# One more pair of chunks as seven block products, tables made once, and a longer split lead in a two-layer decoder kernel

## The chip, the cores and the metric

The kernel runs on one core of a Trainium2 chip. A core has a matrix engine (TensorE, PE in the profile), a vector engine (VectorE, DVE), a scalar engine (ScalarE, ACT), a general engine (GpSimd, POOL) and a queue for transfers (SyncE, SP). Each engine works through its own instructions in order and waits on semaphores for the others. The metric is the time of one execution in microseconds; the kernel before has a median of 1203.88 us over 3 runs (1203.52 to 1204.22).

## The reference

The program is a decoder trunk of two layers over 256 tokens of width 1024. Each layer adds four sub-layers to the residual h, each behind an RMS norm with its own gain:

```python
for l in range(DEPTH):
    h = h + 0.5 * swiglu(rms_norm(h, ffn1_norm[l]), ffn1_w_gate[l], ffn1_w_up[l], ffn1_w_down[l])
    h = h + hybrid_mixer(rms_norm(h, mix_norm[l]), ...)        # state-space groups beside attention
    h = h + memory_cross_attention(rms_norm(h, xattn_norm[l]), rms_norm(mem, mem_norm[l]), ...)
    h = h + 0.5 * swiglu(rms_norm(h, ffn2_norm[l]), ffn2_w_gate[l], ffn2_w_up[l], ffn2_w_down[l])
return rms_norm(h, final_norm)

def swiglu(x, w_gate, w_up, w_down):
    return (jax.nn.silu(x @ w_gate) * (x @ w_up)) @ w_down
```

The feed-forward width is 2816. The state-space part of the mixer has 32 groups of 64 complex states; from its parameters (decay, angle, step size, input and output matrices B and C) the kernel makes tables that depend on no token, and then uses them on all tokens.

## The kernel before, in words

**Precision.** Every large product is made of three: both operands are split into a high part (rounded for the fast matrix format) and a low part (the rest), and high x high, high x low and low x high are summed. So each weight has to be split on the chip. `split_unit` (line 582) makes the high part on ScalarE (`whi`) and the low part on VectorE (`wlo`), in halves of 512 columns, and multiplies by the norm's gain on the way where the plan says so. `split_whole` (line 525) does 1024 columns at once and no gain.

**The stream of weights.** `stream_plan` (line 104) lists every weight unit (128 x 1024) in the order of use. A unit is 12 matmuls of 512 columns: two halves, two blocks of 128 tokens, three products each. SyncE loads units into 4 raw buffers; the split parts have 5 buffers (`N_W`, line 34).

**The planner.** Python code writes all engines' instructions in one order, helped by a small model of time (`Clock`, line 171). TensorE's stream is the main line; everything else (evacuations, transposes, tables, the mixer's chains) is a generator that is resumed when the model's time has come. `feed` (line 503) issues splits ahead of the main line, until a unit is due more than `LEAD` = 4.0 of the model's microseconds later (line 37), or no split buffer is free. One unit is 2.56 of them (`STEP`, line 38, is a half). A generator that yields nothing comes back `MARGIN` = 0.2 after its last operation was to end (line 39).

**Feed-forward stages.** The width is cut into 11 chunks of 256; each has 4 gate/up units and 2 down units. `ffn` (line 857) takes one chunk after the other: the projection into PSUM (`mm`), then silu (`sg`) and the gated product (`g`), four transposes per chunk, a split into `gT`, and the down product into `acc`. `ffn_second` (line 948) is used for the second stage of each layer. There two pairs of chunks (2 and 3, 7 and 8) are made as seven products of blocks instead of eight: a pair is a 2 x 2 block product (token halves and halves of the inner width by two chunks), and with sums and differences of blocks (of the activations in `combos`, line 917, of the weights in `add_block`, line 543, of the products in `pair_step`, line 1010) seven products are enough. One block product is 2 units of 6 matmuls. The order of chunk units (P), block products (S) and down units (D) is written out by hand in `SECOND` (line 51). Since blocks of weights are added before they are split, the norm's gain cannot be in the weights there: `prep` (line 775), which finishes the residual and makes the next stage's input, multiplies it into the activations (`split_gain`, line 470).

**The mixer** (line 1329) projects with 16 w_in units and 12 wkv units; beside that stream run the state's chain (`ssm_states`, line 1373, with two scans and several rotations on VectorE, then `ssm_out`, line 1444, ending in `yT`) and the attention. The chain's result is needed by the units of w_glu.

**The tables** (`ssm_tables`, line 1145) are made once a layer as one generator. It has a small part, some 80 operations on 128 x 16 (exponentials by polynomial, angles, powers, `pw`, `fz`), and a big part: the rotations `rot` and decay `dt`, B scaled (`bbar`), V and its transposes `VT`, the output tables W, and the direct term `ks`, which is copied into `dt` by eight transfers on POOL's queue. For layer 1 it is spawned at 22.0 of the model's time (`START`, line 46), for layer 2 at 12.0 after that layer begins, that is inside its first feed-forward stage. `ssm_states` waits for the whole of it. Scratch tiles of 1024 words come from one pool of 12 (`s4t`, line 396), large table tiles from four named ones, which the pairs' weight blocks X and Y and the combined activations use too.

Of the kernel before, what the change touches and what calls it, by code (L numbers as in the profile page):

```python
# [36 lines left out]
LEAD = 4.0  # L37
STEP = 1.28
# [7 lines left out]
START = (22.0, 34.0)  # L46
# [8 lines left out]
)  # L55
# [13 lines left out]
def second_items():  # L69

    seen = {}
    for item in SECOND.split():
        k = seen[item] = seen.get(item, -1) + 1
        yield item[0], int(item[1:]), k
# [29 lines left out]
def stream_plan():  # L104

    plan = []
    for l in range(L):
# [10 lines left out]
        def second(nm):  # L118
            for kind, j, k in second_items():
                if kind == "P":  # L120
                    plan.append((nm + "_gu", l, 4 * j + k, "A", None, 4 if j == 0 else 1))
                elif kind == "D":
                    plan.append((nm + "_dn", l, 2 * j + k, "B", None, 1))
                else:
                    _, loads, operand, add = PAIR[k]
                    for u in range(2):
                        n = [4 * (j + a) + 2 * b + u for _, a, b in loads]
                        plan.append((nm + "_gu", l, n, "S", ((l, j), u, [x[0] for x in loads], operand, add), 1))
# [7 lines left out]
        ffn("ffn1")  # L136
# [20 lines left out]
    return plan, need  # L157


class Task:  # L160


    def __init__(self, gen, now):
        self.gen, self.t, self.done, self.waiters = gen, now, False, []
        self.pe = -1.0


class Clock:
# [73 lines left out]

    def engine(self, e, cost):
        t = self.cur
        start = max(self.busy[e], t.t + 0.13)
        self.busy[e] = start + cost
        t.t = start + cost
# [113 lines left out]
class Trunk:  # L361
    def __init__(self, ctx, tc, io):
# [21 lines left out]
        self.plan, self.need = stream_plan()  # L384
# [118 lines left out]
    def feed(self, least=-1):  # L503
# [353 lines left out]
    def ffn(self, nm, preps, tail):  # L857
# [4 lines left out]
        def evac(j):  # L862
            def f(t, ps):
# [17 lines left out]
                for f in range(2):  # L881
                    o = f * 256 + t * 128
                    self.p.transpose(p[:, o:o + 128], g[:, f * 128:f * 128 + 128], self.ident)
# [64 lines left out]
    def ffn_second(self, nm, preps, tail):  # L948
# [133 lines left out]
        for kind, j, k in second_items():  # L1082
# [19 lines left out]
            elif kind == "S":  # L1102
                pair_step(j, k)
            else:
# [13 lines left out]
    def exp_acc(self, out, x, n):  # L1118
# [5 lines left out]
        yield  # L1124
        v.tensor_scalar(k, k, -MAGIC, None, op0=ALU.add)
        v.scalar_tensor_tensor(r, k, -0.693359375, r, op0=ALU.mult, op1=ALU.add)
        yield
        v.scalar_tensor_tensor(r, k, 2.12194440e-4, r, op0=ALU.mult, op1=ALU.add)
        v.tensor_scalar(q, r, 1.0 / 5040.0, None, op0=ALU.mult)
        for c in (1.0 / 720.0, 1.0 / 120.0, 1.0 / 24.0, 1.0 / 6.0, 0.5, 1.0):  # L1130
            v.scalar_tensor_tensor(q, q, c, r, op0=ALU.add, op1=ALU.mult)
            yield
        v.tensor_scalar(k, k, 127.0, 0.0, op0=ALU.add, op1=ALU.max)
        v.tensor_scalar(e, k, 8388608.0, None, op0=ALU.mult)
        yield
        v.scalar_tensor_tensor(out, q, 1.0, e.bitcast(F32), op0=ALU.add, op1=ALU.mult)

    def round_(self, out, x):
        self.v.tensor_scalar(out, x, MAGIC, None, op0=ALU.add)
        yield  # L1140
        self.v.tensor_scalar(out, out, -MAGIC, None, op0=ALU.add)
        yield


    def ssm_tables(self, l, tb):
        v, a, g, io = self.v, self.a, self.g, self.io
        t16 = lambda nm: self.sp1.tile([128, 16], F32, tag="p_" + nm, name=nm)

        def cmul(ore, oim, ar, ai, br, bi, t1, t2):
            v.tensor_tensor(ore, ar, br, op=ALU.mult)  # L1150
            v.tensor_tensor(oim, ar, bi, op=ALU.mult)
            yield
            v.tensor_tensor(t1, ai, bi, op=ALU.mult)
            v.tensor_tensor(t2, ai, br, op=ALU.mult)
            yield
            v.tensor_tensor(ore, ore, t1, op=ALU.subtract)
            v.tensor_tensor(oim, oim, t2, op=ALU.add)
            yield

        p = self.sp1.tile([128, 3, 16], F32, tag="sp", name="sp")  # L1160
        g.dma_start(p, io["s5p"][l])
        yield
        b = self.s4t([128, 2, 2, 16, 16], name="bc")
        g.dma_start(b[:, 0], io["s5b"][l])
        g.dma_start(b[:, 1], io["s5c"][l])
        yield
        dc = self.sp1.tile([128, 16], F32, tag="dc", name="dc")
        for e in range(2):
            g.dma_start(dc[64 * e:64 * e + 16, :], io["s5d"][l, e])
        yield  # L1170
        re, im, ldt = p[:, 0, :], p[:, 1, :], p[:, 2, :]
# [4 lines left out]
        yield from self.exp_acc(mag, x1, 16)  # L1176
# [6 lines left out]
        for c in (c1, c2, c3):  # L1183
            v.scalar_tensor_tensor(th, n, -c, th, op0=ALU.mult, op1=ALU.add)
            yield
# [4 lines left out]
        cs, sn = t16("cs"), t16("sn")  # L1190
        v.scalar_tensor_tensor(x1, th, -1.0, th, op0=ALU.mult, op1=ALU.max)
        yield
# [4 lines left out]

        cs_t = self.tab.tile([128, 2, 1024], F32, tag="tC", name="rot")
        d_t = self.tab.tile([128, 2, 1024], F32, tag="tD", name="dt")
        tb.update(cs=cs_t, dtt=d_t)  # L1200
        with self.c.aside():
            g.memset(d_t[:, 1, :], 0.0)
        cidx = self.cst[:, 0:64].unsqueeze(1).to_broadcast([128, 16, 64])
        cmask = self.cst[:, 64:128].unsqueeze(1).to_broadcast([128, 16, 64])
        b3 = lambda z: z.unsqueeze(2).to_broadcast([128, 16, 64])
        v3 = lambda z: z.rearrange("p (m c) -> p m c", m=16)
        v.tensor_tensor(v3(d_t[:, 0, :]), b3(m4), cmask, op=ALU.mult)
        yield
        an, rn = self.s4t([128, 1024], name="ang"), self.s4t([128, 1024], name="rnd")
        v.tensor_tensor(v3(an), b3(fr), cidx, op=ALU.mult)  # L1210
        yield
        yield from self.round_(rn, an)
        v.tensor_tensor(an, an, rn, op=ALU.subtract)
        yield
        v.scalar_tensor_tensor(rn, an, -1.0, an, op0=ALU.mult, op1=ALU.max)
        yield
        a.activation(sn, th, AF.Sin)
        a.activation(cs, x1, AF.Sin, bias=self.halfpi, scale=-1.0)
        a.activation(cs_t[:, 1, :], an, AF.Sin, scale=6.283185)
# [725 lines left out]
```

## Time and profile before

| what | us |
|---|---|
| median of 3 runs | 1203.88 |
| the profiled execution's own time | 1203.8 |
| its span, first to last instruction | 1201.1 |
| TensorE busy in the span | 1187.6 |
| VectorE busy | 903.0 |
| ScalarE busy | 711.9 |
| layer 2's first feed-forward stage, 603.46 to 800.52 | 197.1 |

The profile is one execution. A row of a group gives line, engine, operation, out<-in by the program's names, shapes, count, then busy time, mean ns of one, and the engine's idle time just before. Nearly all engine work is issued by helpers, so the line is mostly the helper's (L345 matmul, L356 transpose, L306 ScalarE, L269 VectorE, L329 POOL) and the names tell the groups apart: `whi` and `wlo` are the split weights, `mm` a projection's PSUM, `acc` a down product's or an output's, `tp` a transpose's or a block product's. The granted clock of TensorE is 0.998 over the span.

### The profile page before, as it was taken

To read this page: it belongs to the slowest core of one execution; us is meant where nothing else is said; L and a number is where in the kernel's file an instruction comes from. 1 tells how busy PE (TensorE), PEld (TensorE's weight loads), DVE (VectorE), ACT (ScalarE), POOL (GpSimd) and SP (SyncE) were. 2 spreads that over 40 slices of the span, in tenths; PEclk is the share of its full clock that TensorE was granted. 3 is DMA by queue.
4 is the path that set the end of the run, shared out by engine and by line. 5 is a ranking of instruction groups with operands and counts; after the bars stand their busy time and mean duration, and the time that the engine had idled before them with its cause. 6 is when DMAs were issued, how large, how long until landed. Compare 5 with 4: busy or idle time off the path is not lost.

```text
span 1201.1 us, 17736 instructions
## 1 busy us (share of the span) xinstructions
PE 1187.6 (99%) x6583; PEld 971.6 (81%) x6583; DVE 903.0 (75%) x1498; ACT 711.9 (59%) x1206; POOL 45.3 (4%) x104
## 2 busy tenths in 40 slices
PE   9999999999999999999999999999999999999997
PEld 7888888777888888888888888888678888888886
DVE  5797776498866688978668879565978675889785
ACT  6665455556856566555465545555687665666553
POOL 2100001000000000000010000100000000000000
PEclk9999999999999999999999999999999999999999
DMA  8656556534644466374565655654436455746542
GB/s 281 212 182 198 161 172 173 173 124 139 193 159 141 156 219 221 128 263 135 176 194 181 192 171 175 186 168 150 140 121 197 158 158 169 294 133 215 191 140 86
DMA packets 59974, 210.91 MB, mean 176 GB/s; under 512 B 7168, under 2 KB 8288, under 8 KB 59888
## 3 DMA queue, kind: packets, MB, share of 16 engines
q1 hardware_dynamic: 56304, 202.92, 52.5%
q0 software_dynamic: 2000, 5.24, 1.5%
q10 hardware_dynamic: 1584, 1.62, 0.5%
q8 instruction: 51, 0.84, 0.3%
q14 instruction: 35, 0.29, 0.1%
HBM read 207.00 MB, written 1.05 MB: 173 GB/s over the span
## 4 chain that ended last, share of the span: by engine, by line
PE 94%; DVE 2%; DMA 1%; ACT 1%; issue 1%; ACTq 0%; POOLq 0%; POOL 0%; DVEq 0%
PE mm L345 48%; PE acc L345 33%; PE tp L345 8%; PE tp L356 5%; DMA uq<-z 1%; DVE wlo L269 1%; DVE p L269 1%; DMA h<-in_x 0%; ACT whi L306 0%; DVE nm L269 0%; ACT junk L306 0%; ACT z L306 0%; ACT up L306 0%; ACTq L315 0%; PE pz L345 0%
## 5 line engine op out<-in xcount | busy, mean ns | idle before, releaser
L269 DVE SCALAR_TENSOR_TENSOR wlo<-raw,gains,whi 128x512 fp32r<-128x512 f32 x368 | 262.8, 746 | 91.8 <-ACT whi L306 90.3
L345 PE MATMUL mm<-whi,xh 128*128 128x512 f32 x768 | 306.9, 400 | 0.0
L345 PE MATMUL mm<-whi,xl 128*128 128x512 f32 x768 | 300.0, 391 | 0.0
L345 PE MATMUL mm<-wlo,xh 128*128 128x512 f32 x768 | 299.1, 390 | 0.3 <-DVE wlo L269 0.3
L306 ACT ACTIVATE whi<-raw,gains 128x512 fp32r<-128x512 f32 x368 | 240.8, 713 | 12.9 <-issue 5.3
L345 PE MATMUL acc<-whi,gT 128*128 128x512 f32 (+1 forms) x704 | 237.3, 397 | 0.0
L269 DVE TENSOR_TENSOR wlo<-raw,whi 128x512 fp32r<-128x512 f32 (+1 forms) x236 | 209.8, 912 | 20.6 <-ACT whi L306 19.5
L306 ACT ACTIVATE whi<-raw 128x512 fp32r<-128x512 f32 (+1 forms) x236 | 181.4, 806 | 45.0 <-DMA raw<-in_wst 17.3
L345 PEld LDWEIGHTS mm<-whi,xh 128*128 128x128 f32 x768 | 144.5, 188 | 31.6 <-issue 1.3
L345 PEld LDWEIGHTS mm<-whi,xl 128*128 128x128 f32 x768 | 144.3, 188 | 30.6
L345 PEld LDWEIGHTS mm<-wlo,xh 128*128 128x128 f32 x768 | 144.6, 188 | 27.9 <-DVE wlo L269 0.6
L345 PEld LDWEIGHTS acc<-whi,gT 128*128 128x128 f32 x704 | 132.0, 188 | 26.2
L345 PE MATMUL acc<-wlo,gT 128*128 128x512 f32 (+1 forms) x352 | 136.9, 389 | 0.0
L345 PE MATMUL mm<-whi,mem 128*128 128x512 f32 x256 | 92.6, 410 | 0.0
L345 PEld LDWEIGHTS acc<-wlo,gT 128*128 128x128 f32 x352 | 66.3, 188 | 11.6
L306 ACT ACTIVATE sg<-mm,rstd 128x256 f32<-128x256 f32 x44 | 20.9, 475 | 86.5 <-PE mm L345 86.4
L306 ACT ACTIVATE gT<-tp 128x512 fp32r<-128x512 f32 x44 | 26.4, 599 | 55.8 <-PE tp L356 55.8
L306 ACT ACTIVATE z<-mm,rstd 128x256 f32<-128x256 f32 (+1 forms) x52 | 29.7, 572 | 48.8 <-PE mm L345 48.0
L345 PEld LDWEIGHTS mm<-whi,mem 128*128 128x128 f32 x256 | 48.1, 188 | 11.5 <-issue 1.3
L345 PE MATMUL mm<-wlo,mem 128*128 128x512 f32 x128 | 51.0, 398 | 3.8 <-DVE wlo L269 3.8
L306 ACT ACTIVATE xh<-tp 128x512 fp32r<-128x512 f32 x32 | 19.1, 598 | 59.2 <-PE tp L356 59.2
L269 DVE TENSOR_TENSOR gT<-tp,gT 128x512 fp32r<-128x512 f32 x44 | 30.3, 688 | 21.2 <-ACT gT L306 21.2
(261 smaller groups left out, 1546.7 us busy)
## 6 DMA issues: line engine op xcount, KB each, us to landing
raw<-in_wst SPq DMA_DIRECT2D x350, 512.0 KB, 4.1
blkX<-in_wst SPq DMA_DIRECT2D x8, 512.0 KB, 4.7
blkP<-in_wst SPq DMA_DIRECT2D x8, 512.0 KB, 7.8
blkY<-in_wst SPq DMA_DIRECT2D x8, 512.0 KB, 8.7
blkQ<-in_wst SPq DMA_DIRECT2D x8, 512.0 KB, 10.2
raw<-in_wst SPq DMA_DIRECT2D x4, 256.0 KB, 5.7
mem<-in_mem POOLq DMA_DIRECT2D x2, 512.0 KB, 7.1
uq<-z ACTq DMA_DIRECT2D x8, 128.0 KB, 4.5
```

Source lines behind the costliest of these rows:

```text
L269: r = getattr(self.e, name)(*a, **k)
L306: r = self.e.activation(out, in_, func, **k)
L345: r = self.e.matmul(out, lhsT, rhs, **k)
L356: r = self.e.transpose(out, in_, ident)
```

## The change

It has four parts. (1) Layer 2's first feed-forward stage is made by `ffn_second`, with an order of its own that has one pair, chunks 2 and 3. Its gain therefore moves from the weights into the activations that layer 1's second stage hands over. (2) The tables' small part is made once, for both layers, on 128 x 32. The big part is cut into three generators; after VectorE operations worth w of the model's time they come back 2.6 w later (`pace`). The first layer's start moves from 22 to 45, the second layer's to the end of the pair's last block product. W is made in two halves of 640 columns instead of five steps of 256. `ssm_states` waits for the first two, `ssm_out` for the third. (3) `feed` takes its lead by unit: 6.0 for feed-forward units from the 17th of a stage on, except the last four, for w_in from the 5th on and for the first 8 wkv units; 4.0 elsewhere. Feed-forward units without a gain are split whole, the down units of the first stages among them. (4) Small edits: the first stage's gated product is written over its silu; the zeroing of every 64th column of the two scans' results goes, and the rotation table gets zeros there instead, by POOL.

```diff
+LEAD_LONG = 6.0
-START = (22.0, 34.0)
+START = (45.0, 34.0)
+PACE = 2.6
...
+SECOND_ONE = (
+    "P0 P0 P0 P0 P1 P1 P1 P1 P4 D0 P4 D0 "
+    "S2 P4 P4 S2 D1 P5 S2 D1 P5 S2 P5 P5 S2 D4 P6 S2 D4 P6 S2 P6 D5 P6 "
+    "D5 D3 P7 D3 P7 D2 P7 D2 P7 D6 P8 D6 P8 P8 P8 D7 P9 P9 P9 P9 D7 P10 P10 P10 P10 D8 D8"
+)
...
-        ffn("ffn1")
+        ffn("ffn1") if l == 0 else second("ffn1")
...
-    return plan, need
+    ahead, at, stage = [], 0, None
+    for nm, l, n, kind, _, skew in plan:
+        at = at + 1 if (nm[:4], l) == stage else 0
+        stage = nm[:4], l
+        long = nm[:3] == "ffn" and at >= 16 and skew == 1 or nm == "w_in" and at >= 4 or nm == "wkv" and n < 8
+        ahead.append(LEAD_LONG if long else LEAD)
+    return plan, need, ahead
...
+    def pace(self):
+
+        if self.cur.dve < 0.5:
+            return self.now
+        w, self.cur.dve = self.cur.dve, 0.0
+        return self.now + PACE * w
...
-            if u >= self.nfree + N_W or (u > least and self.need[u] + q * STEP / 2 > self.main + LEAD):
+            if u >= self.nfree + N_W or (u > least and self.need[u] + q * STEP / 2 > self.main + self.ahead[u]):
                 break
-            self.split_next(self.plan[u][0].startswith("ffn2"))
+            self.split_next(self.plan[u][0].startswith("ffn") and self.plan[u][4] is None or self.plan[u][3] == "S")
...
-                g = self.gp.tile([128, 256], F32, tag="g", name="g")
                 self.a.activation(sg, ps[:, 0:256], AF.Silu, scale=self.r[t])
-                self.v.scalar_tensor_tensor(g, ps[:, 256:512], self.r[t], sg, op0=ALU.mult, op1=ALU.mult)
+                self.v.scalar_tensor_tensor(sg, ps[:, 256:512], self.r[t], sg, op0=ALU.mult, op1=ALU.mult)
...
             elif kind == "S":
                 pair_step(j, k)
+                if then is not None and (j, k) == last:
+                    then()
...
+    def ssm_small(self, z):
+        G = 16 * L
...
+        re, im, ldt = (p[:, i].rearrange("p l m -> p (l m)") for i in range(3))
...
-        yield from self.exp_acc(dt, ldt, 16)
+        yield from self.exp_acc(dt, ldt, G)
...
+    def tab_states(self, l, z, tb):
...
+        yield from self.cmul(vv[0], vv[1], pj(0), pj(1), bh(0), bh(1), *tmp)
...
+    def tab_turns(self, l, z, tb):
...
+        with c.aside():
+            g.memset(cs_t.rearrange("p r (m c) -> p r m c", c=64)[:, :, :, 63:64], 0.0)
+        v.tensor_tensor(v3(d_t[:, 0, :]), b3(m4), cmask, op=ALU.mult)
+        yield c.pace()
+
+    def tab_out(self, l, z, tb):
...
+            v.tensor_tensor(wr, cr, gr, op=ALU.mult)
+            v.tensor_tensor(tmp, ci, gi, op=ALU.mult)
+            yield c.pace()
...
+    def tables(self, l, z, tb, first):
+
+        st = self.c.spawn(self.chain(first, self.tab_states(l, z, tb), self.tab_turns(l, z, tb)), START[0] if l == 0 else None)
+        return st, self.c.spawn(self.chain(st, self.tab_out(l, z, tb)), START[0] if l == 0 else None)
...
-            for x in tables:
-                yield x
-            vt, w, cs, dtt = tb["vt"], tb["w"], tb["cs"], tb["dtt"]
+            yield tables[0]
+            vt, cs, dtt = tb["vt"], tb["cs"], tb["dtt"]
...
-                v.memset(o.rearrange("p (m c) -> p m c", c=64)[:, :, 0], 0.0)
...
             yield states
+            yield tables[1]
...
-        tables = [c.spawn(self.ssm_tables(0, tb), START[0]), c.spawn(self.setup_rest(), START[1])]
+        small = c.spawn(self.ssm_small(z), START[0])
+        tables = self.tables(0, z, tb, small)
...
-            preps = self.ffn("ffn1", preps, prep(0.5))
+            if l == 0:
+                preps = self.ffn("ffn1", preps, prep(0.5))
+            else:
+                tb, tables = {}, []
+                preps = self.ffn_second("ffn1", preps, prep(0.5), lambda: tables.extend(self.tables(l, z, tb, None)))
...
-            preps = self.ffn_second("ffn2", preps, prep(0.5) if l < L - 1 else (lambda t, acc: self.final(t, acc, 0.5)))
+            preps = self.ffn_second("ffn2", preps, prep(0.5, ("ffn1", l + 1)) if l < L - 1 else (lambda t, acc: self.final(t, acc, 0.5)))
```

More of the change, by code (lines that the diff above doesn't have):

```diff
@@ L66, with second_items @@
 EARLY = 3
-def second_items():
+def second_items(nm):
     seen = {}
-    for item in SECOND.split():
+    for item in (SECOND if nm == "ffn2" else SECOND_ONE).split():
         k = seen[item] = seen.get(item, -1) + 1
@@ L246, in engine @@
         self.busy[e] = start + cost
+        if e == "dve":
+            t.dve += cost
         t.t = start + cost
@@ L383, in __init__ @@
         self.dram = P("dram", 1, space=bass.MemoryType.DRAM)
-        self.plan, self.need = stream_plan()
+        self.plan, self.need, self.ahead = stream_plan()
         self.main = 0.0
@@ L1254, in ssm_tables @@
         v.tensor_tensor(f[:, 1, :], f[:, 1, :], x1, op=ALU.mult)
+        yield c.pace()
+        z.update(m4=m4, fr=fr, pw=pw, pr=pr, f=f)
+    def tab_states(self, l, z, tb):
+        v, g, c = self.v, self.g, self.c
+        own = slice(16 * l, 16 * l + 16)
+        f, pr = z["f"][:, :, own], z["pr"][:, :, own]
+        b = tb["b"] = self.s4t([128, 2, 2, 16, 16], name="bc")
+        g.dma_start(b[:, 0], self.io["s5b"][l])
+        with c.aside():
+            g.dma_start(b[:, 1], self.io["s5c"][l])
         yield
-        bb = self.s4t([128, 2, 2, 16, 16], name="bbar")
-        gf = lambda z: z.unsqueeze(2).to_broadcast([128, 16, 16])
-        yield from cmul(bb[:, 0, 0], bb[:, 0, 1], gf(f[:, 0, :]), gf(f[:, 1, :]), b[:, 0, 0], b[:, 0, 1], bb[:, 1, 0], bb[:, 1, 1])
+        bb = tb["bb"] = self.s4t([128, 2, 2, 16, 16], name="bbar")
+        gf = lambda x: x.unsqueeze(2).to_broadcast([128, 16, 16])
+        yield from self.cmul(bb[:, 0, 0], bb[:, 0, 1], gf(f[:, 0, :]), gf(f[:, 1, :]), b[:, 0, 0], b[:, 0, 1], bb[:, 1, 0], bb[:, 1, 1])
         vv = [self.s4t([128, 16, 4, 16], name="V") for _ in range(2)]
@@ L1295, in ssm_tables @@
+    def tab_out(self, l, z, tb):
+        v, g, c = self.v, self.g, self.c
+        pw = z["pw"][:, :, 16 * l:16 * l + 16]
+        b, bb, d_t = tb["b"], tb["bb"], tb["dtt"]
+        w = tb["w"] = self.tab.tile([128, 2, 16, 5, 16], F32, tag="tB", name="W")
         ks = self.s4t([128, 16, 4, 16], name="ks")
         for q in range(2):
+            half = slice(8 * q, 8 * q + 8)
+            wr, wi = (w[:, r, half] for r in range(2))
+            tmp = self.s4t([128, 8, 5, 16], name="Wt")
+            cr, ci = (b[:, 1, r, half].unsqueeze(2).to_broadcast([128, 8, 5, 16]) for r in range(2))
+            gr, gi = (pw[:, r, half].unsqueeze(3).to_broadcast([128, 8, 5, 16]) for r in range(2))
+            v.tensor_tensor(wr, cr, gr, op=ALU.mult)
+            v.tensor_tensor(tmp, ci, gi, op=ALU.mult)
+            yield c.pace()
+            v.tensor_tensor(wr, wr, tmp, op=ALU.subtract)
+            v.tensor_tensor(wi, cr, gi, op=ALU.mult)
+            yield c.pace()
+            v.tensor_tensor(tmp, ci, gr, op=ALU.mult)
+            v.scalar_tensor_tensor(wi, wi, -1.0, tmp, op0=ALU.mult, op1=ALU.subtract)
+            yield
@@ L1845, in setup_mem @@
             yield
-    def setup_rest(self):
-        yield from self.setup_mem(0)
-        yield from self.setup_mem(1)
-        yield from self.setup_bias()
-        yield from self.setup_lam()
     def chain(self, *gens):
         for x in gens:
-            yield from x
+            if isinstance(x, Task):
+                yield x
+            elif x is not None:
+                yield from x
     def run(self):
```

189 lines of the change are left out of this document (84 added, 105 removed).

## The prediction

> **What bounds the kernel now.** I read the page first, then the chain of waits, then what TensorE waits for.
>
> ```profile
> span 1201.1 us, 17736 instructions
> ...
> PE 1187.6 (99%) x6583; PEld 971.6 (81%) x6583; DVE 903.0 (75%) x1498; ACT 711.9 (59%) x1206; POOL 45.3 (4%) x104
> ...
> PE 94%; DVE 2%; DMA 1%; ACT 1%; issue 1%; ACTq 0%; POOLq 0%; POOL 0%; DVEq 0%
> ```
>
> TensorE holds 94% of the chain, VectorE 2%. A busy share alone proves little, since a matmul's record overlaps the next; the chain in order of time says more (start, length, what, count):
>
> ```profile
> 422.07 3.40 PE mm L345 x15
> ...
> 489.83 2.72 PE tp L345 x12
> ...
> 509.85 2.74 PE mm L345 x12
> ...
> 603.46 4.08 PE mm L345 x18
> ...
> 660.81 10.88 PE mm L345 x48
> ...
> 800.52 4.08 PE mm L345 x18
> ```
>
> 48 products of 512 columns in 10.88 us are 0.2267 us each, and one block product of a pair, 12 of them, takes the same 2.72 us. Layer 2's first feed-forward stage runs from 603.46 to 800.52, 197.1 us; layer 1's second stage, with two pairs, from 422.07 to 603.46, 181.4 us. Whether TensorE stands still inside a stage is in the stages' busy times (length, then PE, PEld, DVE, ACT, POOL) and in its waits (total, times, longest):
>
> ```profile
> 208.00:422.00 214.00, 211.52 (x1335) 171.80 (x1334) 152.93 (x255) 138.20 (x272) 7.48 (x17) 1.00 0.50 154
> ...
> 603.00:800.00 197.00, 197.00 (x1110) 160.85 (x1109) 146.01 (x310) 106.88 (x186) 9.59 (x20) 1.00 0.59 181
> 800.00:1014.00 214.00, 211.84 (x1337) 172.13 (x1336) 153.33 (x255) 138.74 (x272) 7.75 (x18) 1.00 0.49 155
> ```
>
> ```profile
> PE mm L345 <- DVE wlo L269: 4.1, 5, 1.4
> ```
>
> The feed-forward stage has no idle TensorE at all: only fewer products shorten it. The idle time in the middle of the program lies in the two mixers, where TensorE waits for the low part of a weight (wlo), which VectorE makes.
>
> [...]
>
> **The change part by part.** *Seven products.* Two chunks cost 2 x 48 = 96 products now; as a pair they cost 7 x 12 = 84. Twelve fewer at 0.2267 us: **-2.72 us**. [...]
>
> A pair also turns each chunk's activations in one group of four transposes where a lone chunk often takes two groups of two. After a group the first product is stretched:
>
> ```profile
> 613.20 0.48 PE L345 MATMUL mm<-whi,xh 128*128 128x512 f32 x1
> 613.51 0.40 PE L345 MATMUL mm<-wlo,xh 128*128 128x512 f32 x1
> ```
>
> 0.31 us to the next start instead of 0.227, so 0.087 us a group; two groups fewer: **-0.17 us** (bounds 0 and -0.35).
>
> *What VectorE and ScalarE do for it.* All rows are mean ns of one after the bar:
>
> ```profile
> L269 DVE SCALAR_TENSOR_TENSOR wlo<-raw,gains,whi 128x512 fp32r<-128x512 f32 x368 | 262.8, 746 | 91.8 <-ACT whi L306 90.3
> ...
> L269 DVE TENSOR_TENSOR wlo<-raw,whi 128x1024 fp32r<-128x1024 f32 x100 | 120.3, 1218 | 9.0 <-ACT whi L306 8.7
> ...
> L269 DVE TENSOR_TENSOR wlo<-raw,whi 128x512 fp32r<-128x512 f32 x136 | 89.5, 688 | 11.6 <-ACT whi L306 10.7
> ...
> L306 ACT ACT_TABLE_LOAD x11 | 14.1, 1283 | 1.8 <-PEq L1935 1.7
> ...
> L269 DVE TENSOR_TENSOR blkX<-blkX,blkP 128x1024 f32<-128x1024 f32 x8 | 9.7, 1218 | 0.0
> ...
> L269 DVE SCALAR_TENSOR_TENSOR ex<-ex 128x16 f32<-128x16 f32 x32 | 5.4, 170 | 0.4
> ```
>
> In that stage VectorE now splits 44 gate/up units in two gain halves (88 x 0.746 = 65.6 us) and 22 down units in two plain halves (44 x 0.688 = 30.3 us). After: 36 plain units, 14 pair units and 22 down units, each whole, 72 x 1.218 = 87.7 us, plus 8 block additions (9.7) and the combinations of the activations and of the products, two 1024-wide and some fifteen 512-wide operations (12.8 by the same rows). The tables' small part, about 80 operations of 0.17 us, leaves layer 2: -13.6. Net 96 to 97 us: VectorE's load in the stage stays near its 146 us in a stage of 194, and the work that hides it is TensorE's own stream. ScalarE gets lighter there. Uncovered, each microsecond that a low part comes late would be one on TensorE. In layer 1 the small part now covers both layers in the same number of operations, twice as wide, and its sines stand apart from the big ones: two more table loads, 2.6 us of ScalarE, which is busy 59%. All of this I cost at 0, between -0.5 and +1.
>
> *The prescaled input.* The second layer's gain moves from the weights to the activations, in eight narrow pairs of operations a token half where there were two. The same treatment is already used at 422.07, where TensorE runs on from one stage to the next as at 603.46. Cost 0.
>
> *Tables later and paced.* In layer 2 their big part starts after the seventh product. In layer 1's second stage that product ends before 509.85, 88 us after the stage's start, so here at about 691. The densest burst is a pair of wide products:
>
> ```profile
> 697.88 2.35 DVE L269 TENSOR_TENSOR V<-pr,bbar 128x1024 f32<-128x1024 f32 x2
> ...
> 763.06 4.41 POOL L329 DMA_DIRECT2D dt<-ks  x8 [147.65 <-DVE wlo L269]
> ```
>
> The pacing leaves 2.6 times a pair's time behind each pair. The big part is about 23 us by the planner's prices: 23 x 2.6 = 60 us and some 10 us of transposes and loads, so it ends near 691 + 74 = 765, as now (763.06), while the mixer's states need it after 820. In layer 1 the same sum puts the end earlier than now. POOL's queue carries the tables' loads and copies beside the row statistics, and those fall at a stage's end, not between 691 and 765. Cost 0.
>
> *The longer lead.* The planner may now put a split 6.0 instead of 4.0 of its microseconds ahead in most feed-forward units, in three of the four w_in chunks and two of the wkv chunks. A unit is 2.56 on its clock and 2.72 on the chip, so 2.0 are **2.13 us** of TensorE time. This meets the mixers' stalls (first layer, then second):
>
> ```profile
> 264.03 0.62 PE L345 MATMUL mm<-whi,mem 128*128 128x512 f32 x2
> 266.06 0.50 PE L345 MATMUL mm<-wlo,mem 128*128 128x512 f32 x1 [1.41 <-DVE wlo L269]
> ...
> 271.52 0.62 PE L345 MATMUL mm<-whi,mem 128*128 128x512 f32 x2
> 272.70 0.50 PE L345 MATMUL mm<-wlo,mem 128*128 128x512 f32 x1 [0.56 <-DVE wlo L269]
> ```
>
> ```profile
> 855.96 0.62 PE L345 MATMUL mm<-whi,mem 128*128 128x512 f32 x2
> 857.92 0.50 PE L345 MATMUL mm<-wlo,mem 128*128 128x512 f32 x1 [1.33 <-DVE wlo L269]
> ...
> 863.40 0.62 PE L345 MATMUL mm<-whi,mem 128*128 128x512 f32 x2
> 864.55 0.51 PE L345 MATMUL mm<-wlo,mem 128*128 128x512 f32 x1 [0.53 <-DVE wlo L269]
> ```
>
> Two starts after 264.03 the product was due at 264.48 and came at 266.06: 1.58 us late. Likewise 0.73, 1.51 and 0.70: 4.52 us in all. What VectorE did meanwhile:
>
> ```profile
> 240.07 0.75 DVE L269 SCALAR_TENSOR_TENSOR wlo<-raw,gains,whi 128x512 fp32r<-128x512 f32 x1 [3.06 <-ACT whi L306]
> ...
> 254.74 4.61 DVE L269 TENSOR_TENSOR_SCAN p<-dt,p 128x1023 f32<-128x1023 f32 x2
> ...
> 260.47 0.74 DVE L269 SCALAR_TENSOR_TENSOR wlo<-raw,gains,whi 128x512 fp32r<-128x512 f32 x1
> ...
> 262.33 0.74 DVE L269 SCALAR_TENSOR_TENSOR wlo<-raw,gains,whi 128x512 fp32r<-128x512 f32 x1
> ...
> 265.27 0.74 DVE L269 SCALAR_TENSOR_TENSOR wlo<-raw,gains,whi 128x512 fp32r<-128x512 f32 x1
> ```
>
> The state's scans and rotations stand between the splits in VectorE's queue; a scan takes 2.3 us where the planner counts 1.1. With 2.13 us more lead one or two low parts move ahead of the scans: the one made at 265.27 gets the place of 262.33, done by 263.07, before its 264.48. The bounds: 0, if VectorE's total work and not its order sets these stalls, and -4.52, all of them. The stalls of one mixer sum to 2.31, the lead is 2.13, and low parts move in whole halves, so I take 2.0 a layer: **-4.0 us**, nearer to the upper bound because VectorE idles 3.06 us ahead of the stretch (240.07) and can make them there.
>
> What is queued behind: the state's chain moves back by up to two low parts, 1.5 us. It ends in
>
> ```profile
> 306.68 1.11 DVE L269 TENSOR_TENSOR yT<-tp,yT 128x512 fp32r<-128x512 f32 x1 [0.22 <-ACT yT L306]
> ```
>
> ```profile
> 315.80 16.33 PE acc L345 x72
> ```
>
> 307.8 against 315.8: 8 us of cover.
>
> Sum: -2.72 - 0.17 - 4.0 = -6.9 us on the profiled 1203.8 us (span 1201.1 and 2.7 around it; the median of the runs, 1203.88, is the same): **1196.9 us**, span about 1194.2.
>
> **The rivals.** *The lead gains nothing*: the mixers' stalls return behind another wide operation, because VectorE is full there. For it: from 254.74 on the rows above show no idle time of VectorE in brackets. Against: the low parts' order, not their sum, fails at 265.27. Time: 1203.8 - 2.9 = 1200.9.
>
> *VectorE becomes the bound in the feed-forward stage*: additions and paced tables hold up low parts and eat the twelve products, while the mixers gain: 1203.8 - 4.0 = 1199.8. Against: layer 1's second stage carries twice the pairs at the same VectorE load with a full TensorE. [...]
>
> *Slower*: the ring of twelve scratch buffers. Pair blocks, two chunks' activations held until their down units, and the tables' eight big tiles now share it in 70 us. A table operation that waits on VectorE for a buffer which TensorE still reads holds all low parts behind it. A buffer is held for up to one chunk, 10.9 us; some 4 us of lead cover it, so a wait costs up to 6.9. It is slower from 6.9 us of such waits in sum; two full ones, before V and Vt, give 1196.9 + 13.8 = 1210.7. Against: the row of V above has no idle time in brackets now.
>
> *Nothing in sum*: new small waits of 6 to 7 us spread over the paced tables give back what is gained: about 1203.5.
>
> **How the numbers follow.** Forecast 0.60 (its own range 1195.0 to 1199.0), lead without gain 0.17, VectorE 0.07, nothing 0.09, slower 0.07. The range 1195.0 to 1201.9 goes from all stalls gone (-2.72 - 0.35 - 4.52, and 1.2 for stretches not looked at) to the first rival with 1 us of new waits. A measurement of this kernel can tell about 0.2%, 2.4 us, from no change: faster means below 1201.5. Faster: 0.60 + 0.07 + 0.11 of the first rival = 0.78; same: the rest of it and "nothing", 0.14; slower 0.08.
>
> **What would show it.** PE instructions 6583 less 12; mm<-whi,xh 768 to 736, tp<-whi,eh 64 to 80; gain halves of wlo 368 to 280, whole ones of raw 100 to 180; 13 table loads; layer 2's first stage 194.2 us; each mixer (now 213.7 and 213.3) 211.5; TensorE's wait for wlo below 1 us. A mixer that keeps its 2.3 us of stalls, a wait for wlo between 610 and 800, or idle time before V on VectorE would prove the forecast's steps wrong.

## The result and the profile after

The changed kernel takes **1193.85 us** (median of 4 runs, 1193.49 to 1193.93); the kernel before, on the same chip, 1204.05 (4 runs, 1203.52 to 1204.32). The ratio is 0.9915, with a 95% interval from 0.9898 to 0.9932: 0.85% faster, well beyond the 0.2% that can be told from nothing. The forecast was 1196.9 with a range from 1195.0 to 1201.9. So the direction is right, but the time lies 1.15 us below the range: the prediction is wrong in size.

From the page of the kernel after:

```profile
span 1192.1 us, 17474 instructions
...
PE 1182.4 (99%) x6571; PEld 967.8 (81%) x6571; DVE 909.7 (76%) x1331; ACT 707.1 (59%) x1141; POOL 46.7 (4%) x104
...
PE 97%; ACT 1%; issue 0%; DMA 0%; DVE 0%; POOLq 0%; POOL 0%; ACTq 0%; DVEq 0%
```

TensorE's share of the chain goes from 94% to 97%, and VectorE's 2% are gone, although VectorE is busier than before. The chain in order of time (start, length, what, count) gives the stages:

```profile
208.03 4.08 PE mm L369 x18
...
418.40 3.40 PE mm L369 x15
...
599.82 3.40 PE mm L369 x15
...
794.41 4.08 PE mm L369 x18
...
1004.80 3.40 PE mm L369 x15
```

| stage | before, us | after, us | difference |
|---|---|---|---|
| start and layer 1's first feed-forward stage | 208.38 | 208.03 | -0.35 |
| layer 1's mixer and cross-attention | 213.69 | 210.37 | -3.32 |
| layer 1's second feed-forward stage | 181.39 | 181.42 | 0 |
| layer 2's first feed-forward stage | 197.06 | 194.59 | -2.47 |
| layer 2's mixer and cross-attention | 213.27 | 210.39 | -2.88 |
| layer 2's second feed-forward stage, to the end of the span | 187.3 | 187.3 | 0 |

The cross-attention alone is 71.72 us long in both layers of both kernels, so the 3.32 and 2.88 us lie in the mixer proper: 141.97 and 141.55 us before, 138.65 and 138.67 after (from the first w_in product to the cross-attention's first product in the trace). These two numbers, and the length of layer 2's first stage, are used for all runs below.

What TensorE waited for (total, times, longest) and the busy times of the three stretches that changed (length, then PE, PEld, DVE, ACT, POOL):

```profile
PE pz L369 <- DVE zero L293: 1.2, 1, 1.2
PE mm L369 <- ACT whi L330: 1.0, 1, 1.0
PE mm L369 <- DVE wlo L293: 0.3, 1, 0.3
PE tp L380 <- DMA h<-in_x: 0.2, 1, 0.2
```

```profile
208.00:418.00 210.00, 209.91 (x1332) 171.30 (x1331) 152.02 (x252) 137.00 (x271) 7.98 (x17) 1.00 0.51 157
600.00:794.00 194.00, 193.88 (x1095) 158.38 (x1094) 151.99 (x181) 103.37 (x139) 8.19 (x16) 1.00 0.56 182
794.00:1005.00 211.00, 210.91 (x1336) 172.13 (x1335) 152.98 (x254) 138.00 (x272) 8.58 (x18) 1.00 0.52 157
```

The wait for wlo fell from 4.1 us to 0.3, and TensorE stands idle for 0.09 us in each mixer stretch, where it was 2.48 and 2.16. The wait of 1.0 for whi is at the program's start (7.30). VectorE's load in layer 2's first stage grew from 146 to 152 us and TensorE kept its stream.

Before, the list of waits had one more that matters, which the prediction had not shown; it is gone after (`up` is ScalarE's copy of the state's input, which a transfer brings):

```profile
PE tp L356 <- ACT up L306: 0.7, 2, 0.5
```

The start's -0.35 is not put down to the change. In the thirteen traces of this case the first stage ends anywhere between 207.32 and 208.64 us, and TensorE's wait for the first input, where it is listed, lies between 0.2 and 0.6 us (0.6 before, 0.2 after).

### The profile page after: what moved, and what is told of

Its sections match the earlier page's. It is cut to its first block, busy times and chain, and to the rows that moved or that the text cites. A ratio compares the mean times of both kernels' runs of the same rounds, so it can differ in the third digit from the quotient of the medians.

```text
span 1192.1 us, 17474 instructions
## 1 busy us (share of the span) xinstructions
PE 1182.4 (99%) x6571; PEld 967.8 (81%) x6571; DVE 909.7 (76%) x1331; ACT 707.1 (59%) x1141; POOL 46.7 (4%) x104
## 4 chain that ended last, share of the span: by engine, by line
PE 97%; ACT 1%; issue 0%; DMA 0%; DVE 0%; POOLq 0%; POOL 0%; ACTq 0%; DVEq 0%
PE mm L369 50%; PE acc L369 33%; PE tp L369 10%; PE tp L380 5%; DMA gains<-in_gains 0%; ACT junk L330 0%; ACT whi L330 0%; DVE h L293 0%; DVE ang L293 0%; ACT on L330 0%; ACT z L330 0%; DVE wlo L293 0%; POOLq L1992 0%; ACT xh L330 0%; POOL rstd L353 0%
## 5 line engine op out<-in xcount | busy, mean ns | idle before, releaser
L369 PE MATMUL mm<-whi,xh 128*128 128x512 f32 x736 | 295.3, 401 | 1.1 <-ACT whi L330 1.0
L293 DVE TENSOR_TENSOR wlo<-raw,whi 128x1024 fp32r<-128x1024 f32 (+1 forms) x228 | 248.0, 1108 | 51.8 <-ACT whi L330 51.1
L369 PE MATMUL mm<-whi,xl 128*128 128x512 f32 x736 | 287.5, 391 | 0.0
L369 PE MATMUL mm<-wlo,xh 128*128 128x512 f32 x736 | 286.9, 390 | 0.3 <-DVE wlo L293 0.3
L330 ACT ACTIVATE whi<-raw 128x1024 fp32r<-128x1024 f32 (+1 forms) x228 | 214.0, 967 | 54.6 <-PE acc L369 25.6
L293 DVE SCALAR_TENSOR_TENSOR wlo<-raw,gains,whi 128x512 fp32r<-128x512 f32 x280 | 198.7, 746 | 53.0 <-ACT whi L330 50.9
L330 ACT ACTIVATE whi<-raw,gains 128x512 fp32r<-128x512 f32 x280 | 184.0, 714 | 10.6 <-PE mm L369 4.6
L330 ACT ACTIVATE z<-mm,rstd 128x256 f32<-128x256 f32 (+1 forms) x70 | 37.8, 547 | 71.7 <-PE mm L369 71.1
L293 DVE TENSOR_TENSOR wlo<-blkX,whi 128x1024 fp32r<-128x1024 f32 x40 | 48.6, 1220 | 9.9 <-ACT whi L330 9.9
L330 ACT ACTIVATE whi<-blkX 128x1024 fp32r<-128x1024 f32 x40 | 42.0, 1055 | 19.5 <-PE mm L369 7.0
```

The costliest lines, as they stand in the source:

```text
L293: r = getattr(self.e, name)(*a, **k)
L330: r = self.e.activation(out, in_, func, **k)
L369: r = self.e.matmul(out, lhsT, rhs, **k)
```

## The experiments

Three theories were put down. **A**: the mixers' 6.2 us come from the longer lead, the feed-forward stage's gain from the pair. **B**: the mixers gain from something else, the tables or the small edits. **C**, formed when A and B had both failed on the first run: the edit of the scans' zeroings costs time at the short lead, so that the lead and this edit cannot be added up.

**Lead back to 4.0, all else as after.**

```diff
-LEAD_LONG = 6.0
+LEAD_LONG = 4.0
```

> The changed kernel with its longer lead taken back: 4.0 everywhere, all else as changed. Theory A (the longer lead alone removes the mixers' waits): both mixers return to about 213.5 us (from 210.4), TensorE's wait for wlo to about 4 us, time 1193.9 + 6 = 1199.9. Theory B (the mixers were freed by the other edits of the state's chain: the strided zeroing dropped, the tables waited for in two steps, the tables out of the way): mixers stay near 210.4, time 1194.

Measured 1208.30 us (4 runs, 1207.85 to 1209.96), ratio to before 1.0043 (1.0028 to 1.0058): not 1200 and not 1194, but slower than the kernel before. Mixers 145.88 and 145.93, layer 2's first stage 194.85. The lead is worth 14.4 us inside the changed kernel, and some other part of the change costs 4 us per mixer without it. Both theories fall as they were put. TensorE's waits name a new one:

```profile
PE tp L369 <- DVE yT L293: 5.4, 2, 2.7
PE mm L369 <- DVE wlo L293: 2.9, 5, 0.7
PE tp L380 <- ACT up L330: 2.2, 2, 1.1
```

**The kernel before with the lead by unit, and nothing else.**

```diff
+LEAD_LONG = 6.0
...
-    return plan, need
+    ahead, at, stage = [], 0, None
+    for nm, l, n, kind, _, skew in plan:
...
+    return plan, need, ahead
...
-            if u >= self.nfree + N_W or (u > least and self.need[u] + q * STEP / 2 > self.main + LEAD):
+            if u >= self.nfree + N_W or (u > least and self.need[u] + q * STEP / 2 > self.main + self.ahead[u]):
```

> The kernel before with nothing but the longer lead by unit (6.0 for the same units as in the change). Theory A: both mixers fall from 213.7 and 213.3 to about 210.5, time 1204.0 - 6 = 1198. Theory B: mixers stay above 213, time 1204.

Measured 1196.72 (4 runs, 1196.32 to 1196.91), ratio 0.9943 (0.9929 to 0.9958): **-7.0 us from the lead alone**. Mixers 138.74 and 138.67, the same as after; the wait for wlo is 0.3 and that for `up` is gone. So A holds for the kernel before, with a larger term than forecast: 6.1 us of it lie in the two mixers.

**The change without the pair** (chunks 2 and 3 plain in layer 2's first stage; prescaled input, pacing of the tables and lead as after; the tables start with chunk 6, since there is no last block product).

```diff
-    "P0 P0 P0 P0 P1 P1 P1 P1 P4 D0 P4 D0 "
-    "S2 P4 P4 S2 D1 P5 S2 D1 P5 S2 P5 P5 S2 D4 P6 S2 D4 P6 S2 P6 D5 P6 "
+    "P0 P0 P0 P0 P1 P1 P1 P1 P2 P2 P2 P2 D0 D0 "
+    "P3 P3 P3 P3 D1 D1 P4 P4 P4 P4 P5 P5 P5 P5 D4 D4 P6 P6 P6 D5 P6 "
...
-                    combo = c.spawn(self.combos(E))
+                    if then is None:
+                        combo = c.spawn(self.combos(E))
...
+                if then is not None and (j, k) == (6, 2):
+                    then()
...
-                if then is not None and (j, k) == last:
-                    then()
```

> The changed kernel with layer 2's first feed-forward stage made of eleven plain chunks (96 products for chunks 2 and 3 instead of 84, no combinations, no block sums), prescaled input, whole splits, tables and lead as changed. If the pair is worth its products: that stage goes from 194.6 to 197.4 us (+2.72 and up to 0.2 of transposes), time 1196.7. If the pair's extra VectorE work costs something there, the stage grows by less than 2.5 us.

Measured 1197.05 (4 runs, 1196.56 to 1197.41), ratio 0.9948 (0.9931 to 0.9964). Mixers as after (138.74, 138.68). The stage, in this run's chain:

```profile
599.57 3.40 PE mm L369 x15
...
797.05 4.08 PE mm L369 x18
```

That is 197.48 us against 194.59 with the pair: **-2.89 us, the forecast's 2.72 + 0.17**. It is also 0.4 longer than the 197.06 before: the prescaled input and the paced tables together cost that much, which the forecast had at 0.

**The longer lead for the mixers alone** (feed-forward units back to 4.0).

```diff
-        long = nm[:3] == "ffn" and at >= 16 and skew == 1 or nm == "w_in" and at >= 4 or nm == "wkv" and n < 8
+        long = nm == "w_in" and at >= 4 or nm == "wkv" and n < 8
```

> The changed kernel with the lead of 6.0 only for w_in and wkv units, 4.0 for all feed-forward units. Theory A in its narrow form (only the mixers use the lead): time and stages as changed, 1193.9, feed-forward stages within 0.2 us of 194.6 and 181.4. If the paced tables need the longer lead too, layer 2's first feed-forward stage grows by 1 us or more.

Measured 1194.32 (4 runs, 1194.04 to 1194.43), ratio 0.9924 (0.9909 to 0.9938); layer 2's first stage 194.90, mixers 138.72 and 138.78. Within the intervals this is the kernel after: the lead in the feed-forward stages does next to nothing. Layer 2's first stage is 0.3 us longer, a little more than the 0.2 that was expected at most.

What of the change costs 4 us per mixer at the short lead? The only edit of the mixer's own work is that of the zeroings: every 64th column of the two scans' results is no longer set to zero on VectorE, the rotation table has zeros there instead.

**The kernel before with this edit alone.**

```diff
+        with self.c.aside():
+            g.memset(cs_t.rearrange("p r (m c) -> p r m c", c=64)[:, :, :, 63:64], 0.0)
...
-                v.memset(o.rearrange("p (m c) -> p m c", c=64)[:, :, 0], 0.0)
...
+            v.memset(xi[:, 0:1], 0.0)
```

> The kernel before with one small edit of the change alone: the two strided zeroings of 128x16 behind the scans go, and POOL puts the zeros into the rotation table instead; lead 4.0. Theory C (at a lead of 4.0 the mixer hangs on where the planner happens to put its pieces, and this edit of 0.15 us moves them so that the state's chain meets the attention in TensorE's queue): both mixer stretches to the output projection's end grow from 141.8 to about 145.9 us, as in the changed kernel without its longer lead; time about 1212. Theory D (that growth came from another part, the tables waited for in two steps or their pacing): the stretches stay at 141.8 or lose 0.1; time 1204.

Measured 1210.05 (2 runs, 1209.55 and 1210.55), ratio 1.0052 (1.0032 to 1.0072); mixers 146.44 and 144.68. **The zeroings' edit alone makes the kernel before 6 us slower**, though it takes work away: the two scans with what stands between them are 4.46 us instead of 4.61, and VectorE's next operation starts 4.37 us after the first scan instead of 5.06. TensorE's waits are those of the first experiment, `yT` for 5.4 us in two waits of 2.7.

**The change at lead 4.0, with the zeroings back.**

```diff
-LEAD_LONG = 6.0
+LEAD_LONG = 4.0
...
-        with self.c.aside():
-            g.memset(cs_t.rearrange("p r (m c) -> p r m c", c=64)[:, :, :, 63:64], 0.0)
...
+                v.memset(o.rearrange("p (m c) -> p m c", c=64)[:, :, 0], 0.0)
...
-            v.memset(xi[:, 0:1], 0.0)
```

> The changed kernel with lead 4.0 everywhere and the strided zeroings put back in place of the zeros in the rotation table. Theory C: the mixer stretches return from 145.9 to about 141.8 us, time 1208.3 - 8.2 = 1200.1. Theory D: they stay at 145.9, time 1208.

Measured 1201.55 (8 runs, 1200.20 to 1201.75), ratio 0.9979 (0.9969 to 0.9989); mixers 142.38 and 141.57, like before (141.97, 141.55); the wait for wlo is back at 3.8 us and that for `yT` is gone. The stretches are those of theory C, the time is 1.4 us above its 1200.1. So C holds, from both sides.

The trace of the first experiment shows how. ScalarE's and then TensorE's rows (start, length):

```profile
290.18 1.09 ACT L330 ACTIVATE yg<-acc 128x512 f32<-128x512 f32 x2 [1.14 <-PE acc L369]
...
292.17 1.28 ACT L330 ACT_TABLE_LOAD   x1
293.46 0.51 ACT L330 ACTIVATE sb<-sb,nm 128x256 f32<-128x256 f32 x1
...
295.44 0.71 ACT L330 ACTIVATE whi<-raw,gains 128x512 fp32r<-128x512 f32 x1
296.06 1.07 ACT L330 ACTIVATE yT<-tp 128x512 fp32r<-128x512 f32 x1
...
297.50 1.06 ACT L330 ACTIVATE yT<-tp 128x512 fp32r<-128x512 f32 x1
```

```profile
293.14 0.60 PE L380 MATMUL tp<-ident,yg 128*128 128x128 f32 x4
...
294.28 0.60 PE L380 MATMUL tp<-ident,yg 128*128 128x128 f32 x4
...
298.29 2.08 PE L369 MATMUL tp<-z,aT 128*128 128x128 f32 x8 [2.72 <-DVE yT L293]
```

The state's chain ends in two groups of transposes (yg), each into a `tp` buffer that only the copy `yT` on ScalarE and its split on VectorE set free. Here both groups are issued by 294.28, but ScalarE is in the middle of one head's softmax: a table load and four exponentials stand in its queue ahead of both copies. The first copy begins at 296.06, 2.3 us after the first group had ended (293.74), and TensorE's next attention product, which needs a `tp` buffer, stands still for 2.72 us, with all products behind it. In the kernel after, the same copies run from 303.93 and 307.92 with only splits ahead of them, and no product waits for them:

```profile
303.93 1.11 ACT L330 ACTIVATE yT<-tp 128x512 fp32r<-128x512 f32 x1
304.80 2.22 ACT L330 ACTIVATE whi<-raw 128x512 fp32r<-128x512 f32 x4
307.92 1.12 ACT L330 ACTIVATE yT<-tp 128x512 fp32r<-128x512 f32 x1 [0.90 <-PE tp L380]
```

The amount of work is nearly the same; the place differs. ScalarE's evacuation of the state's last product (yg) comes 82.75 us after the mixer's first product in the slow kernel, 87.32 us after it in the kernel before and 91.52 in the kernel after. Being early is not what hurts: with a lead of 5.0, tried below, it comes at 85.50 and no product waits for `yT`. What goes with the long wait is its place beside the last two softmaxes of the attention (on 128 x 128 and on 128 x 256). In the slow kernel it stands between the two, so the second one comes ahead of the copies. In the kernel before it stands behind both:

```profile
294.08 1.28 ACT L306 ACT_TABLE_LOAD   x1
295.70 1.09 ACT L306 ACTIVATE yg<-acc 128x512 f32<-128x512 f32 x2 [0.33 <-PE acc L345]
```

The place between them shows in the number of table loads too, since ScalarE then loads a table for the evacuation and another for the softmax behind it (1.28 us each; at 287.75 and 292.17 in the slow kernel's first mixer, where the kernel before has only the one at 294.08): 13 in the program instead of 11. Only three runs have 13: this one, the kernel before with the zeroings' edit, and the last run below, and these are the three in which TensorE stands still for 2.7 us or more behind the copies. By which of its decisions the plan brings the evacuation ahead of the second softmax when 0.15 us go was not taken apart.

Three more runs varied the lead itself: 8.0 for all long units, then 5.0 and 7.0 for the mixers alone (feed-forward units at 4.0, as in the fourth experiment).

```diff
-LEAD_LONG = 6.0
+LEAD_LONG = 8.0
```

> The changed kernel with the longer lead at 8.0 instead of 6.0. If the lead only has to cover the mixers' 3 us of waits, it is already paid out at 6.0, and the five split buffers cap it at four units ahead: mixer stretches 138.7, time 1193.9 within 0.7. If more lead pushes the state's chain back behind the splits, the stretches grow by 1 us or more each.

```diff
-LEAD_LONG = 6.0
+LEAD_LONG = 5.0
...
-        long = nm[:3] == "ffn" and at >= 16 and skew == 1 or nm == "w_in" and at >= 4 or nm == "wkv" and n < 8
+        long = nm == "w_in" and at >= 4 or nm == "wkv" and n < 8
```

> The changed kernel with the longer lead for w_in and wkv units alone, and at 5.0 instead of 6.0. If 6.0 lies on a plateau (the lead covers a shortage of 2 to 3 us of low parts, 1.0 of the planner's microseconds is 1.06 us), 5.0 leaves a part of it: mixer stretches between 139 and 141.8 us, time 1195 to 1200. If the length hangs on how the pieces happen to fall, 5.0 can end anywhere between 138.7 and 146.

The next is the same with 7.0:

> The same with 7.0. Plateau: mixer stretches 138.7 within 0.5, time 1194.3 within 1. Pieces as they fall: anything from 138.7 to 143; at 8.0 for all units the stretches were 140.2.

| lead | median, us (runs) | ratio, 95% interval | mixers, us |
|---|---|---|---|
| 4.0 | 1208.30 (4) | 1.0043 (1.0028 to 1.0058) | 145.88, 145.93 |
| 5.0, mixers | 1197.04 (3) | 0.9941 (0.9919 to 0.9964) | 140.10, 140.10 |
| 6.0, mixers | 1194.32 (4) | 0.9924 (0.9909 to 0.9938) | 138.72, 138.78 |
| 6.0 | 1193.85 (4) | 0.9915 (0.9898 to 0.9932) | 138.65, 138.67 |
| 7.0, mixers | 1195.11 (3) | 0.9925 (0.9903 to 0.9948) | 139.85, 139.36 |
| 8.0 | 1210.14 (4) | 1.0059 (1.0042 to 1.0076) | 140.19, 140.22 |

The mixers have no plateau above 6.0: at 7.0 they are 1.1 and 0.6 us longer, outside the 0.5 that was given for a plateau. In the whole time 7.0 for the mixers cannot be told from 6.0 for the mixers (0.9925 and 0.9924). 5.0 came out as expected, with a part of the waits left. At 8.0 the mixers lose 1.5 us each, as the second of its expectations has it, but the feed-forward stages lose more: layer 1's second stage takes 186.81 us instead of 181.42, layer 2's stages 197.16 and 191.2 instead of 194.59 and 187.3. 8.0 for the mixers alone was not tried. In the feed-forward stages the order changes on two engines. TensorE's waits, its timeline and VectorE's, at lead 8.0:

```profile
PE tp L380 <- DVE z L293: 7.6, 5, 2.5
```

```profile
490.65 0.44 PE L380 MATMUL tp<-ident,z 128*128 128x128 f32 x2 [2.35 <-DVE z L293]
```

```profile
487.78 1.22 DVE L293 TENSOR_TENSOR wlo<-raw,whi 128x1024 fp32r<-128x1024 f32 x1
488.91 1.29 DVE L293 TENSOR_TENSOR qs<-qs 128x512 f32<-128x512 f32 x2
490.12 0.48 DVE L293 SCALAR_TENSOR_TENSOR z<-mm,rstd,z 128x256 f32<-128x256 f32 x1
```

TensorE has to transpose the gated product z, which VectorE makes only at 490.12, behind a 1024-wide low part for a later unit and two combinations of a pair; TensorE stands still for 2.35 us. In the changed kernel, at 6.0, VectorE and then TensorE have:

```profile
487.10 0.48 DVE L293 SCALAR_TENSOR_TENSOR z<-mm,rstd,z 128x256 f32<-128x256 f32 x1
```

```profile
488.71 0.38 PE L380 MATMUL tp<-ident,z 128*128 128x128 f32 x2
```

Counted from the stage's first product, z is made 0.9 us later at 8.0 (69.56 instead of 68.70). The transposes were due 2.7 us earlier (67.58 instead of 70.31): at 6.0 they stand behind the next block product of the pair, at 8.0 ahead of it. So most of this wait comes from TensorE's own order, and the smaller part from the low part ahead of z. Why the step from 6.0 to 8.0 changes just these places was not followed in the plan.

**The kernel before with the scan's true price in the planner.** The prediction had pointed out that a scan takes 2.3 us where the planner counts 1.1. If that error caused the stalls, mending it should remove them.

```diff
-        return self._run("tensor_tensor_scan", width(out), 1.04e-3, out, *a, **k)
+        return self._run("tensor_tensor_scan", width(out), 2.16e-3, out, *a, **k)
```

> The kernel before with the planner's price of a scan set to what the trace shows (2.3 us instead of 1.1 for 1023 elements), lead 4.0, nothing else. If the mispriced scan is what lets the low parts come late, the mixers' waits for wlo fall from 4 us to under 1 and the time to about 1200. If the order in VectorE's queue, set by the short lead, is the cause whatever the price, the mixers stay within 0.5 us of 141.8 and the time at 1204.

Measured 1208.39 (4 runs, 1207.86 to 1208.90), ratio 1.0037 (1.0021 to 1.0052): slower; mixers 145.60 and 144.39. Neither expectation came. The wait for wlo halves, and two other waits take its place, for ScalarE's copies:

```profile
PE mm L345 <- ACT z L306: 3.3, 2, 1.7
PE tp L356 <- ACT up L306: 2.8, 2, 1.7
PE mm L345 <- DVE wlo L269: 1.9, 5, 0.6
```

So a true price does not do what the longer lead does. Whether the wrong one has a part in the stalls of before stays open, since the whole order moved; which decision of the plan puts the two copies late was not taken apart.

**The longer lead without the wkv units** (4.0 for these, else as after).

```diff
-        long = nm[:3] == "ffn" and at >= 16 and skew == 1 or nm == "w_in" and at >= 4 or nm == "wkv" and n < 8
+        long = nm[:3] == "ffn" and at >= 16 and skew == 1 or nm == "w_in" and at >= 4
```

> The changed kernel with the lead of 6.0 for w_in and feed-forward units, but 4.0 for all wkv units. The waits of the kernel before fell on the first wkv units. If these units' own lead is what counts, the stretches go back above 141 us and the time above 1198; if the earlier start through w_in is enough (the queue is then ahead when the scans come), they stay at 138.7 and the time at 1194.

Measured 1207.89 (5 runs, 1207.66 to 1209.11), ratio 1.0038 (1.0022 to 1.0054); mixers 145.70 and 145.91. The wkv units' lead is needed, as the first expectation has it. TensorE's wait, in two pieces of 5.4 us, and VectorE's row behind the first of them:

```profile
PE tp L380 <- DVE sums L293: 10.7, 2, 5.4
```

```profile
297.00 1.09 DVE L293 TENSOR_TENSOR yT<-tp,yT 128x512 fp32r<-128x512 f32 x1 [5.81 <-ACT yT L330]
```

The evacuation of yg stands between the two softmaxes here too (288.71), so the copies `yT` come late on ScalarE and VectorE stands still for 5.81 us. The scaling of the attention's output, which TensorE has to transpose next, is behind both splits `yT` in VectorE's queue and is made at 300.31.

No kernel tried here beats the changed one.

## Why the prediction was wrong, step by step

The forecast's span was 1194.2 us, the measured one is 1192.1. The 2.1 us between them are the lead's term (-6.20 instead of -4.0), the feed-forward stage (-2.47 instead of -2.89) and the start (-0.35, no part of the change): -2.20 + 0.42 - 0.35 = -2.13. The remaining 0.9 of the miss of 3.05 is in the base: the forecast carried the 2.7 us outside the span over to the kernel after, which has 1.8. Of 30 other executions of the kernel before, 27 have 1.8 to 2.0 and three 2.2 to 2.5, so 2.7 is the most that was seen and no good base; the span of 1201.1 is 0.8 us below the mean of the others, 1201.9. That is also most of the reason why the stages in the table add up to 9.0 us and the medians of the runs differ by 10.2. A low end of 1195.0 had no room for either.

- **Seven products: right.** 12 products and two groups of transposes were to give -2.89; with the pair against without it measures -2.89. TensorE's 6571 instructions are 12 fewer, as forecast.
- **VectorE, ScalarE, prescaled input and paced tables at 0: 0.4 us off.** Together they cost 0.4 us in layer 2's first stage (197.48 without the pair against 197.06), inside the -0.5 to +1 given. VectorE's load there is 152 us and not near 146; TensorE's own stream hides it, as argued. One place is seen in the trace: a product due at 728.91, one start of 0.227 us after the one at 728.68, came at 729.18, 0.27 late. The trace names no releaser; what ends just ahead of it, at 729.13, is the first of VectorE's two operations z, which empty the projection's PSUM, and they stand behind one of the tables' operations (ang, from 727.51), 1.22 us long.
- **Two more table loads: wrong.** The count stayed at 11, not 13; nothing hung on it.
- **Tables end near 765: 20 us off, without effect.** POOL's copies of the direct term now run from 784.74 instead of 763.06, since the output tables are paced behind the others. They end at 789.17; the row statistics that follow on POOL start at 792.74, so the cover that the forecast named (their place at the stage's end) has shrunk from 31 us to 3.6.
- **The longer lead: this step failed, in its size.** The mechanism is in the main the one forecast: low parts are made earlier, in time that VectorE had idle (17.0 us from the mixer's first product to the state's first rotation, now 14.4). But they do not move ahead of the scans, as the forecast has it: the same halves stand ahead of the scans in both kernels. Two of them move ahead of the state's first rotation instead. Between that rotation and the scans stood nine halves and now stand seven, both in the kernel after and in the kernel before with nothing but the longer lead. So the scans begin at 252.12 instead of 254.74, which is 2.3 us earlier in the mixer, and all halves behind them come earlier too. The half that before was made at 265.27 and came 1.58 us late, the second in the order of the mem products, is made at 261.96 (the forecast's place was 262.33) and ready at 262.71, 0.7 us ahead of its product at 263.40. VectorE's first rotation before, and then its rows after:

```profile
240.74 2.48 DVE L269 TENSOR_TENSOR p<-acc,rot 128x512 f32<-128x512 f32 x4
```

```profile
238.99 2.48 DVE L293 TENSOR_TENSOR p<-acc,rot 128x512 f32<-128x512 f32 x4
...
250.79 1.42 DVE L293 SCALAR_TENSOR_TENSOR wlo<-raw,gains,whi 128x512 fp32r<-128x512 f32 x2 [1.23 <-ACT whi L330]
252.12 4.46 DVE L293 TENSOR_TENSOR_SCAN p<-dt,p 128x1023 f32<-128x1023 f32 x2
...
261.96 0.75 DVE L293 SCALAR_TENSOR_TENSOR wlo<-raw,gains,whi 128x512 fp32r<-128x512 f32 x1
```

  But the bound of 4.52 was no bound: the term of -4.0 us measures -6.20. The bound held the two large waits for wlo in each mixer and nothing else; all four are gone, and so are a third one of 0.17 us in each mixer and TensorE's wait for ScalarE's `up`, which was in the list of waits and was not read. Before, ScalarE's copy of `up` began at 227.71, and the transposes that use it were due at 228.18, one start after the product at 227.95:

```profile
227.95 0.39 PE L345 MATMUL mm<-whi,xl 128*128 128x512 f32 x1
228.82 1.10 PE L356 MATMUL tp<-ident,up 128*128 128x128 f32 x8 [0.48 <-ACT up L306]
```

  0.64 us late, and 0.39 in layer 2 (820.71 against 820.32). With the longer lead the plan puts these transposes at 229.19 and the copy begins at 226.71, so nothing waits. The lateness of before adds up to 1.58 + 0.73 + 0.17 + 0.64 = 3.12 of the 3.32 us gained in layer 1, and 1.51 + 0.70 + 0.17 + 0.39 = 2.77 of 2.88 in layer 2. The other 0.3 us were not traced.
- **The rivals.** None came. "The lead gains nothing" needed mixers at 213.7 us; they are 210.4. VectorE is not the bound in the feed-forward stage. No idle time stands ahead of V on VectorE. The "slower" rival's mechanism, a wait for a scratch buffer, does not show in TensorE's waits. What can make the kernel slower was not on the list: the zeroings' edit, filed under small edits at no price, costs 6 us by itself, and only the longer lead hides it. With that edit in it and a lead of 4.0 the changed kernel is slower than before; without the edit it gains 2.5 us at 4.0. At 6.0 the edit brings nothing: the mixers are as long without it (138.74 and 138.67). By its own operations, 0.15 us of VectorE, the edit could not have been priced. That the forecast's direction holds all the same is luck in this respect.

## What to carry to other kernels

In a kernel whose engines run queues that were ordered by a plan, an edit is worth what it does to the order, not what its operations cost: here removing 0.15 us of work cost 6 us, and 2 us more lead (of the model's) gave 7 alone and 14 beside that edit. So before bounding what a change of order can bring, add up every wait of the bounding engine in the stretch, the small ones too, and after it try neighbouring values: 4.0 and 8.0 both made the changed kernel slower than the one before. And make the sum against the span, with the time outside it checked against more than one execution.

## What the runs showed of the hardware

In the first experiment a wait of TensorE cost more than its length. Windows of time in its first mixer (length, then PE, PEld, DVE, ACT, POOL, then granted clock, transfer share and GB/s) show the clock after the wait of 2.72 us:

```profile
295.00:298.00 3.00, 0.57 (x3) 0.14 (x1) 1.60 (x2) 3.00 (x7) 0.00 (x0) 1.00 0.17 68
298.00:300.00 2.00, 1.71 (x8) 1.71 (x9) 1.97 (x5) 0.56 (x1) 0.00 (x0) 0.52 0.15 12
300.00:301.00 1.00, 1.00 (x4) 0.83 (x4) 0.93 (x3) 0.60 (x1) 0.00 (x0) 0.50 0.64 180
301.00:302.00 1.00, 1.00 (x5) 0.80 (x4) 0.85 (x3) 0.91 (x6) 0.00 (x0) 0.76 0.78 320
```

The granted clock reads 0.52, 0.50 and 0.76 there and 1.00 again from 302 to 304, and two products start 0.43 us apart (300.59 and 301.02), where 0.23 is the distance at 1.00 (303.52 and 303.75). By these rows the lower clock takes an estimated 0.48 x 2 + 0.50 + 0.24 = 1.70 us off the work. The second mixer's wait, of 2.70 us, is followed by 0.50, 0.50, 0.50 and 0.80 in the windows of 1 us from 892 to 896, by the same sum also 1.70. So of the 7.2 us that each mixer lost there against the kernel after, 5.1 are idle time (2.7 for `yT`, 1.1 for `up`, 1.3 for wlo) and 2.2 are longer busy time, 1.7 of them put down to the clock by this estimate. In the kernel before with the zeroings' edit both mixers have a wait of 2.7 us for `yT`, and the clock falls after the first one only (0.66, 0.50, 0.50 and 0.64 in the windows from 300 to 304; 1.00 in all from 889 to 900). The first mixer is 1.76 us longer than the second (146.44, 144.68), but 0.63 of that is more idle time (its wait for `up` is 1.59 us instead of 0.75), so 1.1 us are left for the clock by this comparison and 1.7 by the windows.

Which wait is followed by the lower clock is not a matter of length alone in these runs. Followed by windows at 0.50 were waits of 2.70 and 2.72 us in the first experiment, both of 5.4 us without the wkv units' lead, one of 2.70 in the kernel before with the zeroings' edit, one of 2.35 at a lead of 8.0, and even one of 1.66 in the kernel with the scan's price (for z, at 301.79). Waits of 2.72, 2.48, 2.35 and 1.66 us elsewhere in the three kernels named last were not (1.00 in the windows behind them), nor were those of up to 1.41 us in the kernel before. What decides was not found.
